# A feed-forward kernel with more groups by seven products and one sum made by an accumulating transfer

## The chip, the cores and the metric

The kernel runs on one core of a Trainium2 chip. The metric is the device time of one execution in microseconds (us). Times given as the median are over three executions without a profile; everything about engines comes from one further execution recorded by the hardware profiler. TensorE (PE) multiplies, VectorE (DVE) and ScalarE (ACT) work elementwise, GpSimd (POOL) and SyncE (SP) here issue transfers, and 16 DMA engines move the data.

## The reference, cut to what matters

Two layers on a 256 x 2048 activation in float32. The first has a gated delta-rule and a linear-recurrence mixer, the second two kinds of attention. Each layer ends in a feed-forward of inner width 5632:

```python
def rmsnorm(x, w):
    y = xf * lax.rsqrt(jnp.mean(xf * xf, axis=-1, keepdims=True) + NORM_EPS)
    return (y * w.astype(jnp.float32)).astype(x.dtype)

def swiglu(hn, w_gate, w_up, w_down):
    return (jax.nn.silu(hn @ w_gate) * (hn @ w_up)) @ w_down

def reference(x, ...):
    h = x
    for layer in range(DEPTH):
        h = h + (gdn_rglru_mixer if layer % 2 == 0 else fox_moba_mixer)(rmsnorm(h, ...), ...)
        h = h + swiglu(rmsnorm(h, ffn_norm[layer]), ffn_w_gate[layer], ffn_w_up[layer], ffn_w_down[layer])
    return rmsnorm(h, final_norm)
```

All weights are float32 in HBM and are read once.

## The kernel before, in words

**Precision.** A float32 operand is kept as two parts in the matmul's own format: `hi`, a cast on ScalarE, and `lo`, the rest, a subtraction on VectorE. A product takes three matmuls: hi by hi, hi by lo, lo by hi. `split` (L176) makes the two parts of a weight tile of 128 x 1024, which `load` (L166) brought by one 512 KB transfer on SP's queue. Raw tiles come from two pools, `wr` with three buffers and, in the feed-forward, `raw4` with four.

**Mixers.** `first` (L210) starts the program: it loads the first four weight columns with the input in ten pieces, and multiplies as they arrive. `wstat` and `xstat` run the later projections. Between them small tasks are advanced by `tick` (L156): a task started with `start(gen, pace)` gets its next step when `pace` ticks have passed. `lru_tile` (L640) is such a task, one for each of eight tiles of the recurrence.

**Feed-forward.** `ffn` (L482) runs eleven blocks of gate and up, 512 columns of each, in stages of four, four and three blocks. Behind each stage come two down blocks (`p` = 0 and 1) over the rows that the stage has produced. A `block` (L409) keeps four sums in PSUM, `F[t][i]`: two halves `t` of the 256 rows by two column groups `i` (gate and up, or two groups of h). Its inner dimension is cut into groups `m` of four 128-row tiles, and each group is computed in one of two ways:

- plainly: four weight tiles, each split, each used for both row halves; 48 matmuls of 128 x 512;
- by sevens (`seven`, L424), in the manner of Strassen and Winograd: seven products in place of eight, 42 matmuls. Three of its weight operands are loaded tiles b11, b22 and b21. Four are sums of loaded tiles: T1 = b11 + b12, T3 = b12 + b22, T2 = T1 + b22, T4 = T2 + b21. `total` (L372) makes a sum on VectorE, then its two parts. The activations' sums are made once by `combine` (L382) for a group and used by all blocks of a stage. Four further banks `M` take products that belong to more than one result, and `ends` (L449) joins them by four sums on VectorE when the last step of the sevens is done.

`groups` (L501) says how many groups of each gate and up block go by sevens: 0, 2, 2, 2 in the first stage, 2 in each later block. Every down block has one. Steps of `seven` are spread between plain units: `lead` and `trail` say how many plain units stand before the first and behind the last step. `hooks` are calls made before plain unit j: transposing the last block's result (`turn`), `combine`, the norm's `rstd`.

After a gate and up block, VectorE adds bank sums to F, ScalarE applies silu, VectorE multiplies, into tiles `fa`. After a down block VectorE adds to h.

**What sets the order.** A planning layer below the program text orders each engine's instructions by its own estimate of when operands are ready and buffers free; each queue then runs in that order. At the end of the last down block the order is written by hand (`second_half`, L1137): final norm, scaling, and output by column groups.

Of the kernel before, what the change touches and what calls it, by code (L numbers as in the profile page):

```python
# [10 lines left out]
D = 2048  # L11
# [36 lines left out]
def body(tc, A, out):  # L48
# [161 lines left out]
    def first(src, n, w):  # L210
# [8 lines left out]
        for a, b in [(k, k + 1) for k in range(4)] + [(k, k + 2) for k in range(4, NK, 2)]:  # L219
            nc.sync.dma_start(xw[a // 4][:, a % 4:a % 4 + b - a], src[:, a:b])  # L220
            if b == 12:
                nc.sync.dma_start(tab[:, 0:NTAB0], A["tab"][:, 0:NTAB0])
                nc.sync.dma_start(col[:, 16:], A["col"][:, 16:])
        for u in range(NK // 2):
            hi = wh.tile([128, 1024], F32R, name="whi")
            lo = wl.tile([128, 1024], F32R, name="wlo")
            for a, b in [(0, 1), (1, 2)] if u < 2 else [(0, 2)]:
                ks = range(2 * u + a, 2 * u + b)
                for k in ks:
                    x = xw[k // 4][:, k % 4, 0:T]  # L230
                    S.activation(X[:, k, 0], x, AF.Copy, scale=w[:, k:k + 1])
                    V.scalar_tensor_tensor(out=X[:, k, 1], in0=x, scalar=w[:, k:k + 1], in1=X[:, k, 0].bitcast(F32),
                                           op0=ALU.mult, op1=ALU.subtract)
                raw = xw[u // 2][:, u % 2 * 2 + a:u % 2 * 2 + b, T:]
                c = slice(512 * a, 512 * b)
                rows = lambda t: t[:, c].rearrange("p (k n) -> p k n", n=n * 128)
                if u == a == 0:
                    V.tensor_copy(rows(hi), raw)
                else:
                    S.copy(rows(hi), raw)  # L240
                V.tensor_sub(rows(lo), raw, rows(hi).bitcast(F32))
                for k in ks:
                    for i, P in enumerate(Ps):
                        ws = slice((k % 2 * n + i) * 128, (k % 2 * n + i + 1) * 128)
                        PE.matmul(P, hi[:, ws], X[:, k, 0], start=k == 0, stop=False)
                        PE.matmul(P, hi[:, ws], X[:, k, 1], start=False, stop=False)
                        PE.matmul(P, lo[:, ws], X[:, k, 0], start=False, stop=k == NK - 1)
# [65 lines left out]
    def sumsq(g, *ts):  # L313
        for t in ts or range(2):
            j = (mx.tile([128, 1024], F32, name="junk", tag="T", bufs=3)[:, 0:512] if more else
# [56 lines left out]
    def total(a, b, name):  # L372

        t = mx.tile([128, 1024], F32, name=name, tag="T", bufs=3)
        V.tensor_tensor(out=t, in0=a, in1=b, op=ALU.add)  # L375
# [4 lines left out]
        return t, (hi, lo)  # L380

    def combine(x4):  # L382

        f = mx.tile([128, 4, T], F32, name="cf", tag="T", bufs=3)
        c = mx.tile([128, 4, 2, 128], F32, name="cc4", tag="T", bufs=3)
        r = fp.tile([128, 2, 4, 2, 128], F32R, name="comb", tag="comb", bufs=3)
# [22 lines left out]
    def block(src, x, comb, nd, hooks, tail=0, lead=2, trail=None):  # L409
# [14 lines left out]
        def seven(m):  # L424
# [5 lines left out]
            yield  # L430
            b12 = load(src(1, 2 * m))
            t, w = total(b11, b12, "T1")
            M[1].add(cx(0), w)
# [12 lines left out]
            F[1][0].add(q(1, 1), total(t, b21, "T4")[1])  # L446
# [35 lines left out]
    def ffn(L, then, fin=None):  # L482
# [18 lines left out]
        for groups in ((0, 2, 2, 2), (2, 2, 2, 2), (2, 2, 2)):  # L501
# [3 lines left out]
            for j in range(piece):  # L505
# [5 lines left out]
                if j == 1 and piece == 3:  # L511
                    hooks.update(late)
                F, e = block(lambda i, u: gu[b, u, i], lambda k: X[:, k], {m: lambda m=m: cx[m] for m in range(groups[j])}, 4, hooks)
                a = [fp.tile([128, 512], F32, name=f"fa{t}", tag="fa", bufs=2) for t in range(2)]
                for t in range(2):
                    if e:
                        V.tensor_tensor(out=a[t], in0=F[t][0], in1=e[t][0], op=(ALU.add, ALU.subtract)[t])
                    S.activation(a[t], a[t] if e else F[t][0], AF.Silu, scale=nrm["rs"][:, t:t + 1])
                for t in range(2):
                    if e:  # L520
                        V.tensor_tensor(out=e[t][1], in0=F[t][1], in1=e[t][1], op=ALU.add)
                    V.scalar_tensor_tensor(out=a[t], in0=e[t][1] if e else F[t][1], scalar=nrm["rs"][:, t:t + 1], in1=a[t],
                                           op0=ALU.mult, op1=ALU.mult)
                    todo.append((hid, j, t, a[t]))
# [71 lines left out]
    def mixer0():  # L596
# [540 lines left out]
    def second_half(add):  # L1137
# [3 lines left out]

        def root(t):

            for i, o in ((2, z[t]), (3, x[t])):
                V.scalar_tensor_tensor(out=o, in0=ssp[:, t, i:i + 1], scalar=1.0 / D, in1=part[:, t:t + 1] if i == 2 else z[t],
                                       op0=ALU.mult, op1=ALU.add)
# [20 lines left out]
        add(1, 0)  # L1167
        root(0)
        sumsq(2, 1)
# [3 lines left out]
        sumsq(3, 1)  # L1173
        ready(0, 2)
        ready(0, 3)
        root(1)
        ready(0, 1)
# [99 lines left out]
```

## Time and profile before

| What | us |
|---|---|
| median of three executions | 2233.04 (2232.82 to 2233.43) |
| profiled execution, device time | 2232.51 |
| its span, first to last instruction | 2230.7 |
| TensorE busy | 2215.9 |
| VectorE busy | 1928.9 |
| ScalarE busy | 1278.9 |
| GpSimd busy | 2.1 |

The clock granted to TensorE was 0.999 of full speed. 420 MB came over SP's queue. The time outside the span is 1.8 us. In the profile's rows, L and a number is the line of the program that made the instruction, `x` and a number counts instructions, and `<-` separates what is written from what is read. For an idle time, `<-` names what ended it. "PEld" are TensorE's weight loads, which run beside its matmuls. Matmul rows overlap their neighbours, so the distance between two starts is the cost of one, not its duration.

### The profile page before, as it was taken

The numbers are of one execution on the slowest core, as the hardware profiler recorded it, in microseconds if no ns is written. First come the engines' busy times: TensorE is split into PE (matmuls) and PEld (weight loads), VectorE is DVE, ScalarE is ACT, GpSimd is POOL, SyncE is SP. The second block draws the span as 40 slices with busy tenths as digits, with TensorE's granted clock in tenths as the row PEclk, the third lists the DMA queues.
The fourth block names the chain that finished last, engine by engine and source line by source line (L and its number), as shares of the span: only waits on it lengthen the run. The fifth ranks groups of instructions, "written<-read, shape, count | busy, mean of one in ns | idle before, by whom it ended". The sixth has DMA issues, their size and how long they took to land.

```text
span 2230.7 us, 30096 instructions
## 1 busy us (share of the span) xinstructions
PE 2215.9 (99%) x11026; PEld 1852.0 (83%) x11026; DVE 1928.9 (86%) x2716; ACT 1278.9 (57%) x1670; POOL 2.1 (0%) x6
## 2 busy tenths in 40 slices
PE   9999999999999999999999999999999999999998
PEld 8888888888888888888878888888888888888886
DVE  8899676789989999899966658857999999999998
ACT  6776664565555665565654444445665466555565
POOL 0000000000000000000000000000000000000000
PEclk9999999999999999999999999999999999999999
DMA  7445445665565666656545455456665666666563
GB/s 280 161 144 168 140 150 187 214 208 195 192 215 196 201 195 203 207 187 200 180 158 175 158 172 172 162 186 217 208 198 191 208 205 203 194 210 202 181 219 131
DMA packets 117780, 422.29 MB, mean 189 GB/s; under 512 B 13152, under 2 KB 14688, under 8 KB 117504
## 3 DMA queue, kind: packets, MB, share of 16 engines
q1 hardware_dynamic: 117344, 420.10, 56.7%
q8 instruction: 86, 1.41, 0.2%
q14 instruction: 62, 0.51, 0.1%
q10 hardware_dynamic: 288, 0.27, 0.0%
HBM read 418.22 MB, written 2.10 MB: 188 GB/s over the span
## 4 chain that ended last, share of the span: by engine, by line
PE 97%; DVE 1%; DMA 1%; ACT 0%; issue 0%; SPq 0%; DVEq 0%; ACTq 0%
PE F L405 16%; PE F L406 16%; PE F L404 16%; PE Pw L199 11%; PE Pw L204 6%; PE Px L303 5%; PE Px L305 5%; PE Px L304 5%; PE M L404 4%; PE M L405 4%; PE M L406 4%; PE Ph L492 1%; PE Psc L1053 1%; PE Pt L326 0%; PE Ps L563 0%; DMA raw<-in_gu 0%
## 5 line engine op out<-in xcount | busy, mean ns | idle before, releaser
L179 ACT CAST whi<-raw 128x1024 fp32r<-128x1024 f32 x724 | 760.7, 1052 | 744.8 <-PE F L406 359.1
L180 DVE TENSOR_TENSOR wlo<-raw,whi 128x1024 fp32r<-128x1024 f32 x724 | 876.5, 1219 | 185.0 <-PE Px L304 74.0
L199 PE MATMUL Pw<-X,whi 128*128 128x512 f32 x1088 | 388.0, 400 | 0.0
L404 PE MATMUL F<-whi,X 128*128 128x512 f32 x848 | 330.5, 391 | 0.0
L405 PE MATMUL F<-wlo,X 128*128 128x512 f32 x848 | 330.4, 390 | 0.0
L406 PE MATMUL F<-whi,X 128*128 128x512 f32 x848 | 330.1, 389 | 0.0
L204 PE MATMUL Pw<-X,wlo 128*128 128x256 f32 x1088 | 304.7, 280 | 0.1
L378 ACT CAST thi<-T 128x1024 fp32r<-128x1024 f32 x208 | 219.1, 1054 | 98.6 <-DVE T L375 71.5
L379 DVE TENSOR_TENSOR tlo<-T,thi 128x1024 fp32r<-128x1024 f32 x208 | 252.5, 1219 | 24.7 <-ACT thi L378 24.2
L199 PEld LDWEIGHTS Pw<-X,whi 128*128 128x128 f32 x1088 | 204.1, 188 | 47.4 <-issue 0.5
L405 PE MATMUL F<-wlo,hid 128*128 128x512 f32 x536 | 208.9, 390 | 0.0
L406 PE MATMUL F<-whi,hid 128*128 128x512 f32 x536 | 208.7, 389 | 0.0
L404 PE MATMUL F<-whi,hid 128*128 128x512 f32 x536 | 208.6, 390 | 0.0
L204 PEld LDWEIGHTS Pw<-X,wlo 128*128 128x128 f32 x1088 | 205.4, 189 | 1.2 <-DVE wlo L180 0.7
L406 PEld LDWEIGHTS F<-whi,X 128*128 128x128 f32 x848 | 159.2, 188 | 33.1
L404 PEld LDWEIGHTS F<-whi,X 128*128 128x128 f32 x848 | 159.2, 188 | 32.7
L405 PEld LDWEIGHTS F<-wlo,X 128*128 128x128 f32 x848 | 159.3, 188 | 32.5
L375 DVE TENSOR_TENSOR T<-raw,raw 128x1024 f32<-128x1024 f32 x98 | 119.2, 1218 | 11.0 <-DMA raw<-in_gu 8.9
L375 DVE TENSOR_TENSOR T<-T,raw 128x1024 f32<-128x1024 f32 x104 | 126.6, 1218 | 1.9 <-DMA raw<-in_dn 1.7
L404 PE MATMUL M<-thi,comb 128*128 128x512 f32 x312 | 121.3, 391 | 0.6 <-ACT thi L378 0.6
L405 PE MATMUL M<-tlo,comb 128*128 128x512 f32 x312 | 121.6, 390 | 0.0
L406 PE MATMUL M<-thi,comb 128*128 128x512 f32 x312 | 121.5, 389 | 0.0
(385 smaller groups left out, 3217.1 us busy)
## 6 DMA issues: line engine op xcount, KB each, us to landing
raw<-in_gu SPq DMA_DIRECT2D x352, 512.0 KB, 4.1
raw<-in_dn SPq DMA_DIRECT2D x176, 512.0 KB, 4.3
raw<-in_w0w SPq DMA_DIRECT2D x72, 512.0 KB, 3.6
raw<-in_wo SPq DMA_DIRECT2D x64, 512.0 KB, 3.5
raw<-in_w1w SPq DMA_DIRECT2D x64, 512.0 KB, 3.6
raw<-in_w1x SPq DMA_DIRECT2D x32, 512.0 KB, 3.6
raw<-in_w0x SPq DMA_DIRECT2D x16, 512.0 KB, 3.6
xw<-in_xw SPq DMA_DIRECT2D x6, 768.0 KB, 10.9
```

The lines of the kernel that those rows point to most:

```text
L179: S.copy(hi, raw)
L180: V.tensor_sub(lo, raw, hi.bitcast(F32))
L199: PE.matmul(P.rearrange("p a b -> p (a b)"), hi[:, kk], X[:, k].rearrange("p a b -> p (a b)"), start=k == 0, stop=False)
L204: PE.matmul(P[:, 0], lo[:, kk], X[:, k, 0], start=False, stop=k == NK - 1)
L303: PE.matmul(Ps[t], x[:, 0, ts], hi[:, kk], start=k == 0, stop=False)
L304: PE.matmul(Ps[t], x[:, 0, ts], lo[:, kk], start=False, stop=False)
L375: V.tensor_tensor(out=t, in0=a, in1=b, op=ALU.add)
L378: S.copy(hi, t)
L379: V.tensor_sub(lo, t, hi.bitcast(F32))
L404: PE.matmul(self.t, xh, hi[:, kk], start=self.i == kk == 0, stop=False)
L405: PE.matmul(self.t, xh, lo[:, kk], start=False, stop=False)
L406: PE.matmul(self.t, xl, hi[:, kk], start=False, stop=kk == 1 and self.i == self.n - 1)
```

## The change

- One more group by sevens in the first gate and up block of each feed-forward (0 becomes 1), with `lead` 6 there; one more in the second down block behind each four-block stage, whose `combine` is called from the first down block's hook 9.
- T3 is no longer summed on VectorE. Once T1 has been formed, GpSimd's queue issues an accumulating transfer that adds b22 from HBM onto the tile of b12 in place; the tile is split later like the other sums. `total` becomes `halves`, which only splits. The other three sums run in one tile, `t`, and each is formed as soon as its operands allow: T1 ahead of the first yield, T2 and T4 right after the previous value has been split. b22 is still loaded and split as an operand.
- Two buffers in place of three for the tag `T`, four in place of three for `comb`. The tiles `fa` are gone: silu and product go into the bank sums' own tiles. First blocks, which had no bank sums, now have them.
- `first` brings the fifth and sixth weight tile as pieces of their own and splits them separately; the first `lru_tile` starts with a pace of 4; in the closing norm the two small sums are moved apart, so that the square root needs only the first.

```diff
-        for a, b in [(k, k + 1) for k in range(4)] + [(k, k + 2) for k in range(4, NK, 2)]:
+        for a, b in [(k, k + 1) for k in range(6)] + [(k, k + 2) for k in range(6, NK, 2)]:
...
-            for a, b in [(0, 1), (1, 2)] if u < 2 else [(0, 2)]:
+            for a, b in [(0, 1), (1, 2)] if u < 3 else [(0, 2)]:
...
-    def total(a, b, name):
-
-        t = mx.tile([128, 1024], F32, name=name, tag="T", bufs=3)
-        V.tensor_tensor(out=t, in0=a, in1=b, op=ALU.add)
+    def halves(t):
+
         hi = fp.tile([128, 1024], F32R, name="thi", tag="thi", bufs=2)
         lo = fp.tile([128, 1024], F32R, name="tlo", tag="tlo", bufs=2)
         S.copy(hi, t)
         V.tensor_sub(lo, t, hi.bitcast(F32))
-        return t, (hi, lo)
+        return hi, lo
...
             b11 = load(src(0, 2 * m))
             M[0].add(q(0, 0), split(b11))
-            yield
             b12 = load(src(1, 2 * m))
-            t, w = total(b11, b12, "T1")
-            M[1].add(cx(0), w)
+
+            t = mx.tile([128, 1024], F32, name="T", tag="T", bufs=2)
+            more_of = lambda a, b: V.tensor_tensor(out=t, in0=a, in1=b, op=ALU.add)
+            more_of(b11, b12)
+
+            G.dma_start(b12, src(1, 2 * m + 1), accum_op=ALU.add)
             yield
             b22 = load(src(1, 2 * m + 1))
             F[0][1].add(cx(3), split(b22))
             yield
-            M[3].add(cx(1), total(b12, b22, "T3")[1])
-            yield
-            t, w = total(t, b22, "T2")
-            M[2].add(cx(2), w)
+            M[1].add(cx(0), halves(t))
+            more_of(t, b22)
             yield
             b21 = load(src(0, 2 * m + 1))
             F[0][0].add(q(1, 0), split(b21))
             yield
-            F[1][0].add(q(1, 1), total(t, b21, "T4")[1])
+            M[2].add(cx(2), halves(t))
+            more_of(t, b21)
+            yield
+            M[3].add(cx(1), halves(b12))
+            yield
+            F[1][0].add(q(1, 1), halves(t))
             yield
...
-        for groups in ((0, 2, 2, 2), (2, 2, 2, 2), (2, 2, 2)):
+        for groups in ((1, 2, 2, 2), (2, 2, 2, 2), (2, 2, 2)):
...
-                    hooks.update(late)
-                F, e = block(..., 4, hooks)
-                a = [fp.tile([128, 512], F32, name=f"fa{t}", tag="fa", bufs=2) for t in range(2)]
+
+                    hooks[6] = late[4]
+                F, e = block(..., 4, hooks, lead=6 if b == 0 else 2, trail=2)
                 for t in range(2):
...
+                    V.tensor_tensor(out=e[t][0], in0=F[t][0], in1=e[t][0], op=(ALU.add, ALU.subtract)[t])
+                    S.activation(e[t][0], e[t][0], AF.Silu, scale=nrm["rs"][:, t:t + 1])
...
                 if p == 0 and piece == 4:
                     hooks.update(late)
+
+                    hooks[9] = lambda hid=hid: ch.update({1: combine(hid[:, 4:8])})
...
-                F, e = block(lambda i, u: dn[2 * p + i, u0 + u], lambda k: hid[:, k], {0: lambda: ch[0]}, piece, hooks, *last)
+                F, e = block(lambda i, u: dn[2 * p + i, u0 + u], lambda k: hid[:, k],
+                             {m: lambda m=m: ch[m] for m in range(1 + (p == 1 and piece == 4))}, piece, hooks, *last)
...
-            start(lru_tile(n, wstat(W[n], True), lw))
+            start(lru_tile(n, wstat(W[n], True), lw), 4 if n == 0 else 2)
...
+        def mean(t, i):
+
+            V.scalar_tensor_tensor(out=(z, x)[i][t], in0=ssp[:, t, 2 + i:3 + i], scalar=1.0 / D,
+                                   in1=z[t] if i else part[:, t:t + 1], op0=ALU.mult, op1=ALU.add)
+
         def root(t):
 
-            for i, o in ((2, z[t]), (3, x[t])):
-                V.scalar_tensor_tensor(out=o, in0=ssp[:, t, i:i + 1], scalar=1.0 / D, in1=part[:, t:t + 1] if i == 2 else z[t],
-                                       op0=ALU.mult, op1=ALU.add)
             S.activation(y[t], ssp[:, t, 3:4], AF.Sqrt, scale=1.0 / D, bias=z[t])
```

More of the change, by code (lines that the diff above doesn't have):

```diff
@@ L314, in sumsq @@
         for t in ts or range(2):
-            j = (mx.tile([128, 1024], F32, name="junk", tag="T", bufs=3)[:, 0:512] if more else
+            j = (mx.tile([128, 1024], F32, name="junk", tag="T", bufs=2)[:, 0:512] if more else
                  mx.tile([128, 512], F32, name="junk", tag="t2", bufs=4))
@@ L511, in ffn @@
                 if j == 1 and piece == 3:
[L512 to L514 removed]
+                    hooks[6] = late[4]
+                F, e = block(lambda i, u: gu[b, u, i], lambda k: X[:, k], {m: lambda m=m: cx[m] for m in range(groups[j])}, 4, hooks, lead=6 if b == 0 else 2, trail=2)
                 for t in range(2):
[L516 to L518 removed]
+                    V.tensor_tensor(out=e[t][0], in0=F[t][0], in1=e[t][0], op=(ALU.add, ALU.subtract)[t])
+                    S.activation(e[t][0], e[t][0], AF.Silu, scale=nrm["rs"][:, t:t + 1])
                 for t in range(2):
[L520 to L522 removed]
+                    V.tensor_tensor(out=e[t][1], in0=F[t][1], in1=e[t][1], op=ALU.add)
+                    V.scalar_tensor_tensor(out=e[t][0], in0=e[t][1], scalar=nrm["rs"][:, t:t + 1], in1=e[t][0],
                                            op0=ALU.mult, op1=ALU.mult)
[L524 removed]
+                    todo.append((hid, j, t, e[t][0]))
                 b += 1
@@ L1167, in second_half @@
         add(1, 0)
+        mean(0, 0)
         root(0)
+        mean(0, 1)
         sumsq(2, 1)
@@ L1173, in second_half @@
         sumsq(3, 1)
+        mean(1, 0)
         ready(0, 2)
@@ L1176, in second_half @@
         root(1)
+        mean(1, 1)
         ready(0, 1)
```

6 lines of the change are left out of this document (3 added, 3 removed).

## The prediction, made before the result was known

> **What bounds the kernel now.** The page's busy times and the chain that ended last come first: nearly the whole span is matmul work, one matmul behind the other.
>
> ```profile
> PE 2215.9 (99%) x11026; PEld 1852.0 (83%) x11026; DVE 1928.9 (86%) x2716; ACT 1278.9 (57%) x1670; POOL 2.1 (0%) x6
> ...
> PE 97%; DVE 1%; DMA 1%; ACT 0%; issue 0%; SPq 0%; DVEq 0%; ACTq 0%
> ```
>
> The shares are means over stages, so the feed-forward stage, where the change acts, is read by windows of 100 us. The columns are the window, then busy us and instructions of PE, PEld, DVE, ACT and POOL, then granted clock, DMA share and GB/s.
>
> ```profile
> 700.00:800.00 100.00, 99.60 (x448) 82.30 (x447) 96.42 (x96) 61.76 (x65) 0.00 (x0) 1.00 0.60 199
> 800.00:900.00 100.00, 100.00 (x451) 82.99 (x450) 96.82 (x104) 56.11 (x60) 0.00 (x0) 1.00 0.60 199
> 900.00:1000.00 100.00, 100.00 (x447) 82.89 (x446) 92.22 (x93) 54.60 (x55) 0.00 (x0) 1.00 0.60 201
> ```
>
> TensorE is never idle, but VectorE is 92 to 97% busy beside it: two engines at their limit. GpSimd does nothing, and the DMA engines are 60% busy. A busy matmul row says 0.39 us, but matmuls overlap, so the price of one is the distance between starts, in the timeline:
>
> ```profile
> 738.01 0.39 PE L404 MATMUL F<-whi,X 128*128 128x512 f32 x1
> ...
> 752.06 0.39 PE L406 MATMUL F<-whi,comb 128*128 128x512 f32 x1
> ```
>
> These are first and last of 63 matmuls, 62 steps in 14.05 us: 0.2266 us each. VectorE's work on a tile of 128x1024 is priced the same way:
>
> ```profile
> 744.10 1.23 DVE L180 TENSOR_TENSOR wlo<-raw,whi 128x1024 fp32r<-128x1024 f32 x1
> ...
> 753.19 1.22 DVE L379 TENSOR_TENSOR tlo<-T,thi 128x1024 fp32r<-128x1024 f32 x1
> ```
>
> That is first and last of nine in a row, eight steps in 9.09 us: 1.137 us each. How near VectorE is to holding TensorE up shows in a rare matmul that had to wait for it, and in the waits, where ScalarE by contrast mostly waits for TensorE to free a buffer (total us, times, longest):
>
> ```profile
> 759.87 0.50 PE L405 MATMUL F<-tlo,X 128*128 128x512 f32 x1 [0.40 <-DVE tlo L379]
> ```
>
> ```profile
> ACT whi L179 <- PE F L406: 359.1, 267, 3.3
> ...
> DVE T L375 <- DMA raw<-in_gu: 8.9, 13, 1.8
> ```
>
> **Six more groups by sevens.** A plain group is 4 tiles x 2 row halves x 6 = 48 matmuls, a group by sevens 7 x 6 = 42. The first block of each feed-forward gains one, and so does the second down block of each of its two four-block stages: 3 per feed-forward, 6 in all, 36 matmuls. TensorE loses 36 x 0.2266 = **8.16 us**. All of it is on the path, provided that the other engines keep up in these six blocks.
>
> **Does VectorE keep up?** These groups price its work (busy us, then mean ns of one):
>
> ```profile
> L378 ACT CAST thi<-T 128x1024 fp32r<-128x1024 f32 x208 | 219.1, 1054 | 98.6 <-DVE T L375 71.5 <-PE M L406 23.6 <-PE F L406 1.8
> L379 DVE TENSOR_TENSOR tlo<-T,thi 128x1024 fp32r<-128x1024 f32 x208 | 252.5, 1219 | 24.7 <-ACT thi L378 24.2
> ...
> L375 DVE TENSOR_TENSOR T<-T,raw 128x1024 f32<-128x1024 f32 x104 | 126.6, 1218 | 1.9 <-DMA raw<-in_dn 1.7
> L375 DVE TENSOR_TENSOR T<-raw,raw 128x1024 f32<-128x1024 f32 x98 | 119.2, 1218 | 11.0 <-DMA raw<-in_gu 8.9
> ...
> L453 DVE TENSOR_TENSOR e<-M,e 128x512 f32<-128x512 f32 x128 | 84.8, 683 | 1.7 <-PE M L406 1.4
> ...
> L539 DVE TENSOR_TENSOR e<-h,e 128x512 f32<-128x512 f32 x48 | 30.8, 682 | 0.0
> L546 DVE TENSOR_TENSOR h<-F,e 128x512 f32<-128x512 f32 x44 | 29.5, 683 | 1.3 <-PE F L406 1.3
> L522 DVE SCALAR_TENSOR_TENSOR fa<-e,rs,fa 128x512 f32<-128x512 f32 x40 | 29.0, 745 | 0.0
> ...
> L392 DVE TENSOR_TENSOR comb<-cc,comb 128x1024 fp32r<-128x1024 f32 x10 | 12.2, 1220 | 0.3
> ...
> L390 DVE TENSOR_TENSOR cc<-cf,cc 128x256 f32<-128x256 f32 x20 | 8.3, 417 | 0.0
> ```
>
> Before, a group by sevens has 3 splits, 4 sums and 4 splits of sums on VectorE: 11 x 1.137 = 12.5 us against 42 x 0.2266 = 9.5 us of matmuls. A plain group has 4 x 1.137 = 4.5 us against 10.9. So a group by sevens is VectorE's burden, paid for by plain groups beside it. The change takes one sum of the four to a transfer: 10 x 1.137 = 11.4 us.
>
> A block of two and two, by rows: before, (2 x 11 + 8) x 1.137 = 34.1 us, and 4 bank sums, 4 gate sums and 2 of the transposed result at some 0.60 (0.68 less the 0.08 by which 1.219 exceeds 1.137), and 2 gate products at 0.66: 7.3. Together 41.4 us, in a block that takes 42.4:
>
> ```profile
> 736.60 0.87 PE Ph L492 x8
> 778.99 0.87 PE Ph L492 x8
> ```
>
> That is 98%, as the windows say. After: 28 x 1.137 + 7.3 = 39.1 us, 92%. Second down block of a four-block stage, now two and two: 31.8 + 12 x 0.60 = 39.0 us against 180 x 0.2266 = 40.8. First down block, one and three, with both combines in it: 22 x 1.137 + 14 x 0.60 + 2 x (1.22 + 4 x 0.42 + 1.22) = 41.6 against 186 x 0.2266 + 1.7 of transposes = 43.9. First block, one and three: 25.0 + 7.3 - 1.2 + 2 x 4.1 + about 1 for the norm = 40.3 against 42.1. Each fits, by 4 to 5%, so I take no loss; what pays for it is the sums taken away. If these still went over VectorE, the down block would need 41.3 of 40.8.
>
> ScalarE gets three more casts per new group and four more of combine: 22 x 1.05 = 23 us. At 57% busy it has the room. The four combines' VectorE work is counted above.
>
> **The sum by a transfer.** 58 accumulating transfers of 512 KB are added on GpSimd's queue, which nothing else uses there. The transfer waits for the first sum (it overwrites an operand of it), and cast and subtraction of its result wait for it. Its price shows nowhere in the trace. The nearest rows:
>
> ```profile
> raw<-in_gu SPq DMA_DIRECT2D x352, 512.0 KB, 4.1
> raw<-in_dn SPq DMA_DIRECT2D x176, 512.0 KB, 4.3
> ```
>
> Lower end 4.1 us, a plain load of the size; upper end three of these, 12.3 us, for it reads HBM, reads SBUF and writes SBUF. I take 7 us, under two loads (8.2), because the engines are only 60% busy and the second stream is on chip.
>
> What hides it: the order of the changed program puts 8 to 27 VectorE instructions between the first sum and the subtraction that uses the transfer; at row prices 9.1 to 23.2 us, 16 of the 58 under 12. ScalarE's queue is stricter: behind the waiting cast stand casts of other tiles, which VectorE wants next. Counting the casts at 1.05 us each, the transfer must be in within 5.2 to 7.5 us in some 14 cases, within 10 in 18, and later in the other 40. At 7 us the overruns are at most 1.8 us each, in some nine blocks that each have 3.3 us to spare. So 0 on the path. If the cover goes, what is late next is ScalarE's cast, then every cast behind it, then TensorE.
>
> Traffic: 58 x 512 KB is 11% more in the two stages, 22% if each costs double: the DMA share goes from 0.60 to 0.73 at most. Plain loads share these engines and may land later. The changed order holds one raw buffer longer and another shorter; counting VectorE's work between a buffer's release and its next use, 18 of 528 loads have under 4 us, before 28. Taken at zero; above it stands the 8.9 us that VectorE already waited there, without TensorE stopping for more than the row quoted.
>
> [...]
>
> **Sums ahead of splits, one running sum, two T buffers, gate in place, hooks.** Same instructions in another order. A combine needs both T buffers, and every hook that calls one stands behind the last step of a group by sevens (position 9 or 10 after step 7 at 7 or 8; 6 after 4). Gate tiles are now the bank sums' own, read by the next block's transposes at unit 2, rewritten after unit 4. Cost 0, hidden by these distances.
>
> **Three small edits.**
>
> ```profile
> 12.12 0.38 PE L245 MATMUL Pw<-X,whi 128*128 128x256 f32 x1 [0.65 <-ACT whi L240]
> ...
> PE Pgate L645 <- ACT cx L582: 0.6, 1, 0.6
> ...
> 2221.77 1.41 DVE L1159 SCALAR_TENSOR_TENSOR fin<-h,fin,fin 128x512 f32<-128x512 f32 x2
> ...
> 2223.09 0.42 DVE L1145 SCALAR_TENSOR_TENSOR fin<-ssp,fin 128x1 f32<-128x1 f32 x2
> 2223.34 0.29 ACT L1147 ACTIVATE fin<-ssp,fin 128x1 f32<-128x1 f32 x1 [0.73 <-DVE fin L1145]
> ```
>
> Finer first pieces remove up to 0.65; two more casts and one more issue come back, so 0.4. The first recurrence tile's later step removes its 0.6. At the end the square root no longer waits 0.73 for two small sums that stand behind two products on VectorE; the products keep VectorE until 2223.1 anyway, so 0.3 of it. Together **1.3 us**.
>
> **The sum.** The profiled execution took 2232.5 us (span 2230.7 and 1.8 around it), 0.5 under the median of 2233.04. 2232.5 - 8.16 - 1.3 = 2223.0; set against the median 2223.6. I say **2223.6 us**.
>
> **Rivals.**
>
> *Late transfers: slower.* [...] At 12.3 us the 18 tight cases overrun by 5 us on average, 90 us; in some 14 blocks 3.3 each is absorbed, 46; 44 lost less the gain of 9.5: about 2268 us. [...] Against: GpSimd's queue is empty, and most uses stand 12 us and more away.
>
> *Late in part: a smaller gain.* At 8.5 us and loads at 5, some 4 us are lost: about 2227.5.
>
> *VectorE sets the pace: no change.* If the transfers cost VectorE some 0.05 us an instruction, its work in the down blocks passes TensorE's (40 x 0.05 makes 41.0 of its 39.0, against 40.8), and matmuls saved become waits: only the small edits stay, 2233.0 - 1.3, about 2231.7. For: four to five per cent of room. Against: 41.4 of 42.4 was fed without stops.
>
> **How the numbers follow.** A change of less than 0.2% (4.5 us) is about what a measurement of this kernel can't tell from none. My forecast, 2218 to 2227: 0.58. In part: 0.13. No change: 0.09. Slower: 0.20. So faster 0.71, same 0.09, slower 0.20. The likeliest case's own range is 2218 (a few more of the short waits gone) to 2227; the range reaches over the smaller gain, no change and the first of the slower, 2218 to 2240, and leaves the late transfers out.
>
> **What would show it.** Right: 36 matmuls fewer at the same 0.2266 us; PE idle no more than 15 us; VectorE nearer 92 than 97% in the gate blocks; accumulating transfers landing within 8 us; Pgate's wait gone. Wrong: waits of the cast of the transferred sum, PE waiting for such a cast, plain loads at 6 us or more, or VectorE rows above 1.22 us.

## The result and the profile after

The changed kernel takes **2246.61 us** (median of six, 2243.82 to 2247.91) where the kernel before takes 2233.19: a ratio of 1.0058, 95% interval 1.0045 to 1.0071. It is 13.4 us slower; 2223.6 was forecast, and 2240 was the end of the range. The profiled execution took 2246.88 us with a span of 2245.1.

The page after, busy times, then the chain that ended last, then GpSimd's data queue (packets, MB, share of 16 engines):

```profile
PE 2219.3 (99%) x10990; PEld 1842.4 (82%) x10990; DVE 1942.5 (87%) x2741; ACT 1294.9 (58%) x1695; POOL 52.3 (2%) x64
...
PE 91%; DVE 4%; DMA 3%; issue 1%; ACT 1%; DVEq 0%; ACTq 0%
...
q0 software_dynamic: 8352, 30.41, 8.2%
```

The 36 matmuls are gone (11026 to 10990), but the chain is no longer all TensorE: 97% has become 91%, and VectorE and loads stand in it. The windows shown of before, now:

```profile
700.00:800.00 100.00, 100.00 (x447) 81.62 (x446) 94.53 (x94) 60.92 (x65) 4.31 (x5) 1.00 0.76 229
800.00:900.00 100.00, 98.68 (x442) 80.93 (x441) 93.75 (x102) 55.11 (x58) 2.59 (x3) 1.00 0.69 214
900.00:1000.00 100.00, 99.40 (x438) 80.58 (x437) 95.30 (x97) 57.82 (x59) 5.17 (x6) 1.00 0.77 229
```

VectorE is a little less busy in two windows and more in the third, the DMA engines are at 0.69 to 0.77 in place of 0.60, and TensorE now loses up to 1.3 us of a window. Its waits for the subtraction of a sum (total us, times, longest), before and then after:

```profile
PE F L405 <- DVE tlo L379: 0.4, 1, 0.4
```

```profile
PE F L403 <- DVE tlo L377: 8.3, 10, 1.4
```

Beside these 8.3 us it waits 3.3 more in the feed-forward after the change, for the two parts of a plain tile. VectorE's sums wait for loads not much longer in all than the 8.9 us shown of before:

```profile
DVE T L431 <- DMA raw<-in_gu: 10.7, 10, 1.7
```

The landing times (KB, median us), where the loads of gate and up tiles had 4.1:

```profile
raw<-in_gu SPq DMA_DIRECT2D x352, 512.0 KB, 4.6
...
raw<-in_gu POOLq DMA_DIRECT2D x42, 512.0 KB, 6.7
```

By stage, from the first matmul of one to the first of the next, the span grew by 14.4 us. GU is a stage of gate and up blocks, DN the two down blocks behind it:

| After less before, us | GU 1 | DN 1 | GU 2 | DN 2 | GU 3 | DN 3 |
|---|---|---|---|---|---|---|
| matmuls saved, forecast | -1.36 | -1.36 | 0 | -1.36 | 0 | 0 |
| first feed-forward | +4.0 | +0.1 | +2.2 | -0.2 | +0.8 | 0.0 |
| second feed-forward | +2.9 | 0.0 | +2.4 | +0.5 | +1.9 | -1.1 |

Two places show how it is lost. The first is a block's end. Here is the timeline of SP, VectorE and TensorE there; the SPq row covers two load issues, the first at 678.92 and the last 10.3 us later. Then the chain that released VectorE's sum (start, us, what):

```profile
678.92 10.60 SPq L173 DMA_DIRECT2D raw<-in_gu  x2
...
680.11 1.23 DVE L431 TENSOR_TENSOR T<-raw,raw 128x1024 f32<-128x1024 f32 x1 [1.21 <-DMA raw<-in_gu]
...
681.85 1.22 DVE L377 TENSOR_TENSOR tlo<-T,thi 128x1024 fp32r<-128x1024 f32 x1
...
683.12 0.50 PE L403 MATMUL F<-tlo,hid 128*128 128x512 f32 x1 [0.92 <-DVE tlo L377]
```

```profile
674.09 1.15 DVE wlo L180
675.25 4.76 DMA raw<-in_gu
680.11 1.23 DVE T L431
```

The next block's first sum stands in VectorE's queue ahead of the last subtraction of this one; it waits 1.21 us for a load, and TensorE waits 0.92 for the subtraction. That load, of b12, was issued when the subtraction of an ordinary tile had freed its buffer, and took 4.76 us. Nine of the ten waits above, 8.0 of the 8.3 us, are this chain, each with such a load, of 4.1 to 5.2 us (median 4.8). In the kernel before the sum stands there at ten block ends, too, with loads of 3.5 to 4.5 (median 3.9); it waits at most 0.78, and TensorE stops once, for 0.40.

In the same stretch SP's queue issues nothing for 10.3 us, because its next buffer isn't free. SP's waits for a buffer, before and then after, show it in the longest of them:

```profile
SPq L173 <- DVE wlo L180: 1425.7, 571, 6.8
```

```profile
SPq L173 <- DVE wlo L180: 1375.0, 555, 10.1
```

Counted over the feed-forwards' load issues, none before was over 8 us behind the last; after there are eight. But each of the eight stands behind the buffer of an ordinary tile, when seven tiles of the next block are loaded already. They are no loss of lead.

The second place is the first block of a feed-forward, where only the three buffers of `wr` are in use for the first twelve loads:

```profile
447.65 11.60 SPq L173 DMA_DIRECT2D raw<-in_gu  x4
...
448.20 1.00 POOL L434 DMA_DIRECT2D raw<-in_gu  x1 [421.10 <-DMA raw<-in_gu]
...
456.59 1.04 ACT L179 CAST whi<-raw 128x1024 fp32r<-128x1024 f32 x1 [2.69 <-DMA raw<-in_gu]
```

```profile
450.45 6.06 DMA raw<-in_gu
```

```profile
457.68 0.50 PE L402 MATMUL F<-whi,X 128*128 128x512 f32 x1 [0.89 <-ACT whi L179]
458.94 0.50 PE L403 MATMUL F<-wlo,X 128*128 128x512 f32 x1 [0.76 <-DVE wlo L180]
...
459.91 0.63 PE L403 MATMUL F<-wlo,X 128*128 128x512 f32 x1
460.34 0.63 PE L404 MATMUL F<-whi,X 128*128 128x512 f32 x1
```

Four loads in 11.6 us. The one that the cast waits for was issued beside the transfer, as soon as an ordinary subtraction had freed one of the three buffers, and took 6.06 us; the load at this place in the second feed-forward took 6.7, and without transfers 3.5 and 3.7 (e1 below). The cast waits 2.69 for it, TensorE waits, and then runs 0.43 us a matmul for 3 us (the last section).

### The profile page after: what moved, and what is told of

It reads as the page before. It is cut to its first block, busy times and chain, and to the rows that moved or that the text cites. A ratio compares the mean times of both kernels' runs of the same rounds, so it can differ in the third digit from the quotient of the medians.

```text
span 2245.1 us, 30395 instructions
## 1 busy us (share of the span) xinstructions
PE 2219.3 (99%) x10990; PEld 1842.4 (82%) x10990; DVE 1942.5 (87%) x2741; ACT 1294.9 (58%) x1695; POOL 52.3 (2%) x64
## 4 chain that ended last, share of the span: by engine, by line
PE 91%; DVE 4%; DMA 3%; issue 1%; ACT 1%; DVEq 0%; ACTq 0%
PE F L403 14%; PE F L402 14%; PE F L404 14%; PE Pw L199 11%; PE Pw L204 5%; PE Px L303 5%; PE Px L305 5%; PE Px L304 5%; PE M L403 4%; PE M L402 4%; PE M L404 4%; DMA raw<-in_gu 3%; DVE wlo L180 1%; DVE T L431 1%; DVE tlo L377 1%; PE Ph L496 1%
## 5 line engine op out<-in xcount | busy, mean ns | idle before, releaser
L179 ACT CAST whi<-raw 128x1024 fp32r<-128x1024 f32 x718 | 750.5, 1052 | 687.6 <-PE F L404 329.7
L402 PE MATMUL F<-whi,X 128*128 128x512 f32 x820 | 321.6, 392 | 1.5 <-ACT whi L179 1.5
L404 PE MATMUL F<-whi,X 128*128 128x512 f32 x820 | 320.0, 390 | 0.0
L376 ACT CAST thi<-T 128x1024 fp32r<-128x1024 f32 x174 | 183.0, 1052 | 134.2 <-DVE T L431 97.0
L377 DVE TENSOR_TENSOR tlo<-T,thi 128x1024 fp32r<-128x1024 f32 x174 | 211.8, 1218 | 15.0 <-ACT thi L376 14.4
L402 PE MATMUL F<-whi,hid 128*128 128x512 f32 x480 | 187.6, 391 | 0.0
L404 PE MATMUL F<-whi,hid 128*128 128x512 f32 x480 | 187.0, 390 | 0.0
L403 PE MATMUL F<-wlo,hid 128*128 128x512 f32 x480 | 186.9, 389 | 0.0
L402 PEld LDWEIGHTS F<-whi,X 128*128 128x128 f32 x820 | 154.3, 188 | 32.6 <-ACT whi L179 2.3
L431 DVE TENSOR_TENSOR T<-T,raw 128x1024 f32<-128x1024 f32 x116 | 141.4, 1219 | 0.8
L404 PE MATMUL M<-thi,comb 128*128 128x512 f32 x348 | 135.4, 389 | 0.0
L402 PE MATMUL M<-thi,comb 128*128 128x512 f32 x348 | 135.4, 389 | 0.0
L403 PE MATMUL M<-tlo,comb 128*128 128x512 f32 x348 | 135.4, 389 | 0.0
L404 PEld LDWEIGHTS F<-whi,hid 128*128 128x128 f32 x480 | 90.1, 188 | 18.8
```

Source lines behind the costliest of these rows:

```text
L179: S.copy(hi, raw)
L376: S.copy(hi, t)
L377: V.tensor_sub(lo, t, hi.bitcast(F32))
L402: PE.matmul(self.t, xh, hi[:, kk], start=self.i == kk == 0, stop=False)
L403: PE.matmul(self.t, xh, lo[:, kk], start=False, stop=False)
L404: PE.matmul(self.t, xl, hi[:, kk], start=False, stop=kk == 1 and self.i == self.n - 1)
```

## The experiments

All times are medians; the ratio is to runs of the kernel before made beside them.

| Run | us | ratio, 95% interval |
|---|---|---|
| changed kernel | 2246.61 | 1.0058, 1.0045 to 1.0071 |
| e1 sum on VectorE | 2237.51 | 1.0019, 1.0009 to 1.0028 |
| e2 counts as before | 2255.88 | 1.0097, 1.0082 to 1.0112 |
| e3 first block plain | 2243.31 | 1.0044, 1.0029 to 1.0058 |
| e4 seven buffers earlier | 2241.12 | 1.0035, 1.0020 to 1.0049 |
| e5 = e1 and e4 | 2232.06 | 0.9994, 0.9985 to 1.0004 |
| e6 = e5, steps in the old order | 2235.55 | 1.0009, 1.0000 to 1.0018 |
| e7 transfers without sum | 2241.59 | 1.0040, 1.0025 to 1.0054 |
| e8 = e5, first block plain | 2237.04 | 1.0016, 1.0007 to 1.0025 |
| e10 = e5, transfers in the third stage | 2234.06 | 1.0001, 0.9991 to 1.0010 |
| e12 before, small edits alone | 2233.62 | 1.0000, 0.9991 to 1.0009 |
| e13 = e4, transferred sum used earlier | 2282.23 | 1.0215, 1.0202 to 1.0229 |
| e14 = e5, combine early in third block | 2239.30 | 1.0024, 1.0014 to 1.0033 |
| e15 = e5, combine late in third block | 2231.47 | 0.9991, 0.9982 to 1.0000 |
| e16 = e5, groups as before | 2241.91 | 1.0036, 1.0023 to 1.0050 |
| e17 = e16, idle transfers | 2242.70 | 1.0041, 1.0026 to 1.0056 |
| e18 = e5, buffer held longer | 2239.06 | 1.0033, 1.0020 to 1.0046 |
| e21 transfers, groups as before | 2251.39 | 1.0088, 1.0073 to 1.0103 |
| e20 = e21, target off the rings | 2236.92 | 1.0021, 1.0011 to 1.0031 |

**One part undone at a time.** The first theory (A in the expectations) was that the transfers and their late loads lose the time; its rival, that the added groups overload VectorE and ScalarE.

```diff
 e1
-            G.dma_start(b12, src(1, 2 * m + 1), accum_op=ALU.add)
 ...
             F[0][1].add(cx(3), split(b22))
+            V.tensor_tensor(out=b12, in0=b12, in1=b22, op=ALU.add)
 e3 (and e2, which also takes the second group from the down blocks)
-        for groups in ((1, 2, 2, 2), (2, 2, 2, 2), (2, 2, 2)):
+        for groups in ((0, 2, 2, 2), (2, 2, 2, 2), (2, 2, 2)):
 e4
-        loads[0] = -12
+        loads[0] = -4
```

> The changed kernel with T3 summed on VectorE again, in place on the tile of b12, and no accumulating transfers; all else stays. Theory A (late loads: the transfers' traffic and the long hold on b12's buffer make weight tiles land late, and a sum or cast that waits for one holds up its whole queue): the stalls go with the transfers, 2224 to 2236 us, though VectorE works 58 x 1.14 = 66 us more. Theory B (VectorE is short of time in the blocks that gained a group): more work on VectorE makes it worse, 2250 us or more.

> The changed kernel with the number of groups by sevens as before: none in the first blocks, one in every down block. The transfers (52 of them), the order of the sums and the small edits stay. Theory A: the first blocks' loss of about 9.7 us is gone, the down blocks' 6 us of gain and 6 of loss cancel, about 2240 us, so still above the kernel before. Theory B: 2233 us or less, for VectorE then has less to do than in the kernel before.

> The changed kernel with plain first blocks; the second down blocks keep their two groups by sevens. Theory A: the first blocks' stages took 4.0 and 2.9 us longer than before though each has 6 matmuls less; without them 2239 to 2241 us. Theory B: the down blocks are the burden, at most 2 us less than the changed kernel, 2244 us or more.

> The changed kernel with the four buffers of raw4 in use from the fifth load of each feed-forward and not from the thirteenth, so that the first block's group by sevens has seven raw buffers and not three. Theory A: the first blocks' stalls of 3 to 5 us each go, and with them the half clock behind them, 2237 to 2240 us. Theory B: no effect, within 1 us of 2246.6.

Putting the sum back on VectorE gains 9.1 us, although VectorE gets 58 instructions more, and the four down stages with two groups in their second block now take 0.75 to 1.4 us less than before: these groups pay. Using the four buffers of `raw4` from the fifth load on gains 5.5. Both times lie just above theory A's ranges (by 1.5 and 1.1 us) and far from its rival's (e1), or between the two (e4). The first blocks' groups cost 3.3 us with the transfers (e3, between the two expectations). e2 missed on both: taking the down blocks' second group away, too, made 12.6 us *more*, lost in single waits of up to 5.2 us in the first block of the second stages. So fewer groups by sevens are no repair, and that wait is taken up below.

**Both repairs, the order, and half the traffic.** e5 joins e1 and e4; e6 has the old order of steps with sums in place; e7 leaves the accumulation out of the transfer; e8 is e5 with a plain first block.

```diff
 e7
-            G.dma_start(b12, src(1, 2 * m + 1), accum_op=ALU.add)
+            G.dma_start(b12, src(1, 2 * m + 1))
 e6
             M[0].add(q(0, 0), split(b11))
+            yield
             b12 = load(src(1, 2 * m))
             ...
+            M[1].add(cx(0), halves(t))
             yield
             b22 = load(src(1, 2 * m + 1))
             F[0][1].add(cx(3), split(b22))
             yield
+            V.tensor_tensor(out=b12, in0=b12, in1=b22, op=ALU.add)
+            M[3].add(cx(1), halves(b12))
+            yield
             more_of(t, b22)
+            M[2].add(cx(2), halves(t))
             ...
```

> VectorE forms b12+b22 and the fourth raw buffer ring is in use from the fifth load on. If the two repairs mend different places, their gains add: 2246.6 - 9.1 (sum on VectorE) - 5.5 (ring earlier) = about 2232 (2230 to 2234). If they mend the same place (casts of the first block waiting for a load), little is added to the first of them: 2234 to 2237.

> As the run with both repairs, but each group's steps in the order of before (every sum formed just ahead of its own split, sums in place, no transfers). If the order of the steps (a next block's first sum ahead of the last step's subtraction in VectorE's queue) is what the third stage loses, the stages of gate and up come back from +1.8 and +3.4 us against before to about 0 and the whole comes to 2222 to 2228. If the order is harmless and VectorE simply has too much to do with one more group per stage, it stays within 1.5 us of the run with both repairs.

> The changed kernel with transfers that copy and do not accumulate (b12 then holds b22 alone, so the third middle sum is left out of the result): the same 58 issues, waits, buffers and landings' order, but half the traffic if accumulating reads the target too. If the loss by the transfers is DMA engine time (3.2 us of 16 engines each, against 1.6), their share of the engines halves and the time lies half way to the run with the sum on VectorE: 2239 to 2243. If it is the buffer that they hold and the wait for their landing, it stays at 2245 to 2248.

> As the run with both repairs, but the first block of each feed-forward layer without a group by sevens (two groups fewer, 12 matmuls or 2.7 us more). If the groups in the first blocks pay as matmuls saved, 2.7 us above the run with both repairs. If they cost what they save there (casts and sums at a block whose loads have only begun), within 1 us of it or below.

The two gains add (14.6 us), but by stages they overlap: the first stages, at +4.0 and +2.9 in the changed kernel, are at +0.7 and +1.0 in e1, +1.3 and +0.2 in e4, +0.6 and -0.2 in e5. That they mend different places isn't shown. The old order is 3.5 us slower, outside both expectations: without transfers, sums ahead of splits are no fault of the change; beside transfers this doesn't show it. The first blocks' groups, a loss of 3.3 us in the changed kernel, are worth 5.0 here, more than the 2.7 of their matmuls; the rest isn't explained. Without the accumulation the transfer takes 4.1% of the engines in place of 8.2%, lands in 4.7 us in place of 6.7, and 5.0 us come back, as expected of traffic.

**Traffic or the held buffer?** From the start of the sum b11 + b12 to the end of the subtraction of the transferred sum, b12's raw buffer is held 19.1 us in the changed kernel (median of the 56 groups whose sum is in the trace), as long in e7, and 11.5 in e1. So e7's gain came without a shorter hold. The transfer itself lands a median of 8.5 us before its cast starts. How long SP's queue stands behind that buffer can be read: a load into it waits for the transferred tile's subtraction (L377). The changed kernel, then e5, which has no transfers:

```profile
SPq L173 <- DVE tlo L377: 72.3, 56, 3.4
```

```profile
SPq L173 <- DVE tlo L377: 133.8, 56, 4.3
```

The queue stands behind it for less time in all than without transfers, at most 3.4 us at once. e13 tests the hold all the same and moves the use of the sum forward, on the base of e4. e12 and e10 settle two smaller terms.

```diff
 e13
             M[1].add(cx(0), halves(t))
             more_of(t, b22)
             yield
+            M[3].add(cx(1), halves(b12))
+            yield
             b21 = load(src(0, 2 * m + 1))
             ...
-            M[3].add(cx(1), halves(b12))
-            yield
 e10 (block gets dma = piece == 3)
+            if dma:
+                G.dma_start(b12, src(1, 2 * m + 1), accum_op=ALU.add)
 ...
+            if not dma:
+                V.tensor_tensor(out=b12, in0=b12, in1=b22, op=ALU.add)
```

> The changed kernel with the early ring, and the step that splits the transferred sum moved ahead of the load of b21, so that its raw buffer is free some two steps sooner. The traffic is the same. If SP's queue standing behind that held buffer is what makes the loads late, the issue gaps over 8 us go and the time falls from 2241.1 to 2234 to 2238. If the traffic alone does it, 2240 to 2242.

> VectorE forms b12+b22 and the ring of raw buffers starts early as before in these runs, but the six groups of each third stage (12 of 58) use the accumulating transfer. In the third stage VectorE lost 2.8 and 2.0 us against before, and the kernel with transfers and the early ring only 0.2 and 0.3. If a transfer helps where VectorE is the limit and costs elsewhere, 2232.1 - 2.6 - 1.7 = 2227.8 (2226 to 2229.5). If transfers cost wherever they stand, 2232 or more.

> The kernel before with the small edits alone (finer first pieces, first recurrence tile at pace 4, the closing norm's small sums moved apart). By the prediction 1.3 us: 2231.8. By the trace of the changed kernel (start 0.8 later, the gate's wait moved to another producer, 0.2 at the end) nothing: 2233.1 to 2233.9.

e13 missed both expectations, by 40 us. The hold fell to 13.9 us and the long issue gaps from nine (e4) to two, but now the casts stand for the landing. ScalarE's waits of e13; the changed kernel has no row of this kind:

```profile
ACT thi L376 <- DMA raw<-in_gu: 134.8, 31, 6.4
```

So the hold can't be shortened this way: it is the cover of the landing, and the run can't part the two theories. e10 lies in the second range expected of it, 2232 or more: in the third stages it lost 4.4 and 2.0 us against before, no less than e5, mostly in `PE F L402 <- ACT thi L376` (3.2 us in all); why the transfers help there in e4 and not here was not found. The small edits alone are worth nothing.

**Traffic alone, and the hold taken away.** e16 is e5 with the groups as before and three `comb` tiles, which leaves room for a tile that nothing reads; e17 adds accumulating transfers into it, each behind the same first sum. e21 is e16 without the marker and with the real transfers; e20 gives b12 two tiles of its own, so that SP's queue never meets a raw buffer that a transfer holds; it also adds two buffers to the seven, and no run adds buffers without taking b12 off the rings.

```diff
 e16 and e17
             more_of(b11, b12)
+            V.tensor_copy(scr[0][:, 0:1], t[:, 0:1])
 e17 only
+            G.dma_start(scr[0], src(1, 2 * m + 1), accum_op=ALU.add)
 e20 against e21
-            b12 = load(src(1, 2 * m))
+            b12 = mx.tile([128, 1024], F32, name="b12", tag="b12", bufs=2)
+            nc.sync.dma_start(b12, src(1, 2 * m))
```

> Groups as before (no group in the first blocks, one in every down block), VectorE forms b12+b22 in place, early ring, the steps in the new order, and one VectorE copy of a 128x1 column per group as a marker. Baseline for the run beside it. The two runs with both repairs put the down groups at -1.1 to -1.4 us in each of four stages: 2237.0 + 5 = about 2242 if nothing else moves; 2233 to 2236 if the order of steps costs nothing against before.

> The run beside it with an accumulating transfer of 512 KB per group (52) into a tile that nothing reads, issued behind the marker, at the place where the changed kernel issues its own. Buffers and steps are the same; only traffic and GpSimd's issues are added. If traffic makes plain loads late and TensorE wait, 4 to 10 us above the run beside it, with plain loads at 4.9 us or more beside a transfer. If only the raw buffer held longer costs, within 1 us of it.

> Groups as before, accumulating transfers into the loaded tile of b12, early ring. The baseline for the next run. Between the run with counts as before (2255.9) and that less the early ring's gain of up to 5.5: 2248 to 2256.

> The same, with b12 in two tiles of its own, outside the seven raw buffers that SP's queue fills in turn. Transfers, traffic and waits for their landing stay; what goes is that a load in SP's queue waits for the buffer that a transfer holds. If that held buffer is the cost, the time falls to that of the idle transfers, 2240 to 2244, with no issue gaps over 8 us. If the use of the transferred sum is the cost, it stays within 2 us of the run beside it.

Windows of e16, then of e17:

```profile
700.00:800.00 100.00, 100.00 (x448) 81.89 (x447) 96.35 (x101) 60.22 (x64) 0.00 (x0) 1.00 0.62 197
```

```profile
700.00:800.00 100.00, 100.00 (x448) 81.92 (x448) 96.46 (x101) 60.63 (x65) 4.33 (x5) 1.00 0.76 223
```

The same 0.76 of the DMA engines as in the changed kernel, plain loads later in the mean of the feed-forwards (4.3 to 4.6 us), and TensorE not idle. The two medians differ by 0.8 us, within their intervals. Traffic alone is not the cause; but here the first sum stands ahead of the last subtraction at two block ends only, in the changed kernel at ten. With b12 off the rings, 14.5 us come back, to 2236.92: below the 2240 to 2244 expected, and 5.0 below e16, which has no transfers at all. So this edit takes away more than the transfers cost, and its gain is no measure of a held buffer. TensorE's waits in the feed-forward, all of them, of e21:

```profile
PE F L402 <- ACT thi L376: 8.3, 3, 4.0
...
PE F L403 <- DVE tlo L377: 2.7, 4, 1.3
```

and of e20:

```profile
PE M L403 <- DVE tlo L377: 0.6, 1, 0.6
```

Where the longest of these arises, in windows of 5 us, e21 first, then e20 at the same work, from one window earlier:

```profile
700.00:705.00 5.00, 5.00 (x24) 4.08 (x22) 3.33 (x3) 1.06 (x1) 0.00 (x0) 1.00 0.95 248
705.00:710.00 5.00, 1.04 (x4) 0.62 (x3) 0.74 (x1) 2.76 (x3) 0.00 (x0) 0.84 0.65 261
```

```profile
695.00:700.00 5.00, 5.00 (x24) 4.14 (x23) 3.30 (x4) 2.88 (x3) 0.00 (x0) 1.00 1.00 261
700.00:705.00 5.00, 5.00 (x23) 4.01 (x22) 3.42 (x3) 3.93 (x4) 0.00 (x0) 1.00 0.91 361
705.00:710.00 5.00, 5.00 (x23) 3.94 (x22) 4.34 (x5) 2.37 (x4) 0.00 (x0) 1.00 0.23 54
```

The DMA engines saturate in both (0.95 and 1.00), when loads follow close behind an accumulating transfer; those loads then take 6.2 to 8.6 us in both. In e20 TensorE still has tiles ahead of it: the load of b21 was issued at 691.83 and took 4.3. In e21 it was issued at 698.52, when an ordinary tile's subtraction had freed its buffer, took 8.6, and TensorE stops for 4 us. e2's waits of up to 5.2 us stand at the same work. The changed kernel has no stop of this length.

Late landings that cost nothing elsewhere reach TensorE where the loads have no lead. In the changed kernel that is at two places. In the first blocks, the early ring (e4) cuts the first stages' losses of 4.0 and 2.9 us to 1.3 and 0.2 (its second stages lose 3.6 and 5.8 in place of 2.2 and 2.4), and half the transfers' engine time under the same hold (e7) cuts them to 1.1 and 0.3. At the block ends, 8.0 us of waits are the chain shown above. TensorE's waits for a sum's subtraction fall from 8.3 to 5.9 us in e7; e1, where no first sum stands ahead of a last subtraction, has none of the chain. (e1's 9.1 us come from both places, less 4.6 that its third stages lose more.) There the sum's place alone costs little (0.4 us in the kernel before; 0.6 in e20, where it stands so at 23 block ends), and later loads alone cost nothing that can be told (e17: 0.8 us, within the intervals). Why the planner puts the sum there, and how much of each stop is the later landing, was not measured.

**Holding longer without a transfer, and the third stage.** e18 puts the split of b12 + b22 last. e14 and e15 move the third stage's `combine`, which the change had moved to unit 6 of the second block.

```diff
 e18
-            M[3].add(cx(1), halves(b12))
-            yield
             F[1][0].add(q(1, 1), halves(t))
             yield
+            M[3].add(cx(1), halves(b12))
+            yield
 e15 (e14: hooks[1])
-                if j == 1 and piece == 3:
+                if j == 2 and piece == 3:
                     hooks[6] = late[4]
```

> The run with both repairs, without transfers, and the split of b12+b22 moved behind the last sum's, so that b12's raw buffer is held one step longer. If a held buffer alone makes loads late and TensorE wait, 2235 to 2242 with issue gaps over 8 us. If it takes the transfer as well, 2231 to 2233.

> The run with both repairs (sum on VectorE, early ring), and in the third stage the combine for the down blocks called before unit 1 of the third block instead of unit 6 of the second. If that combine, standing among the bank sums at the end of the second block, is what the third stage loses (2.8 and 2.0 us against before), the time falls by about 4 to 2228 (2227 to 2229.5). If the order of the steps loses it, 2231 to 2233.

> The same with the combine before unit 6 of the third block, again at the end of a block. If a place at the end of a block is what costs, no gain: 2231 to 2233. If only the second block was the wrong one, 2228.

e18 came out at the time that a held buffer would give, with seven long issue gaps, but its trace doesn't support the reading. VectorE's rows there:

```profile
1019.63 1.51 DVE L523 TENSOR_TENSOR e<-F,e 128x512 f32<-128x512 f32 x2
1021.05 1.22 DVE L390 TENSOR_TENSOR comb<-cc,comb 128x1024 fp32r<-128x1024 f32 x1
```

A weight's subtraction stands behind bank sums and the combine, and TensorE waits 3.1 us for it, once in each third stage: 6.2 of its 7.1 us of waits in the feed-forward. The planner had ordered VectorE otherwise, and none of TensorE's waits goes back to a load, though b12's buffer is held 19.4 us, as long as in the changed kernel. A hold without a transfer didn't make loads late for TensorE here.

e5 loses 2.8 and 2.0 us in the third stages. With the combine at the end of the third block it is 1.9 and 0.9; the median gains 0.6 us, as much as can be told from none. At that block's start it costs 7.2 us, which neither expectation had: the end of a block as such is not the bad place, though e15's time lies in the range named for that. What the third stages still lose was not settled. e15, the fastest run here, is 0.9991 of before, 0.9982 to 1.0000: a kernel with all the added groups and no transfer comes out even.

## Why the prediction was wrong

**The step that failed** is in *The sum by a transfer*: "Plain loads share these engines and may land later", taken at zero, because "above it stands the 8.9 us that VectorE already waited there, without TensorE stopping for more than the row quoted". The loads do land later, a median of 4.6 us in place of 4.1, and VectorE's waits for them grow only to 10.7 us. But the step took such waits as harmless wherever they fall. At nine block ends they now fall on a sum directly ahead of the subtraction that TensorE is due, and it stops for 8.0 us in all; the row quoted was the one such stop of before, 0.40. Taking the transfers out brought 9.1 us, first blocks included (e1). The same paragraph's count of a raw buffer held longer was no fault: it is held 19.1 us in place of 11.5 (e1), and SP's queue stands behind it 72 us in place of 134 (e5). *Sums ahead of splits* took the order at "Cost 0, hidden by these distances" and looked at the combines and gate tiles, not at this sum. The split of the 8.0 us between the landing and the order stays open.

**"Each fits, by 4 to 5%, so I take no loss"** failed for the first block: it priced VectorE and ScalarE and not the three buffers there, which give a load of 6.1 to 6.7 us no lead. With the early ring the two first stages get 5.5 us back (e4).

**"If these sums still went over VectorE, the down block would need 41.3 of 40.8"** was too dark: in e5, with these sums on VectorE, the four stages still gain 1.05 to 1.36 of the 1.36 us forecast. The transfers were not needed there.

**Matmuls**: right, 36 fewer at 0.2266 us. In the first stages e5 takes +0.6 and -0.2 us against before, e15 -0.3 and -1.0.

**The transfer's price**: right. 7 us were taken, 6.7 measured, and no cast waited for one. **Traffic at zero**: right by itself (e17: 0.8 us, within the intervals), wrong where the later loads have no lead.

**Small edits, 1.3 us**: zero (e12). In the changed kernel's one profiled execution the first matmul came at 5.52 us, before at 4.74, in e12 at 4.81; the finer pieces brought nothing. The gate's wait only moved to another producer:

```profile
PE Pgate L650 <- ACT V L837: 0.8, 1, 0.8
```

**Hooks at cost 0**: the combine at unit 6 of the second block costs some 2 us by stages (e5 to e15), though the median moves by 0.6 only, which can't be told from none.

**Rivals.** Late transfers was not the case: none of the changed kernel's casts waited for one. In e13 they did, and it took 41 us more than e4. That 44 were forecast is chance, for that was for a landing of 12.3 us, and the transfers of e13 landed in 6.8. VectorE's rows stayed at 1.22 us, so no cost of the transfers to VectorE shows. Nor does a delay of GpSimd's transfers beside a busy VectorE: in e4 all 58 issue 1.5 to 1.8 us after the first sum begins, which itself takes 1.22, and in the changed kernel, whose VectorE is 94 to 95% busy in the windows shown, 56 do so within 2.1 (median 1.75).

**The sum again.** From 2246.6 the sum on VectorE and the early ring together take 14.6 (e5), the combine 0.6 (e15): 2231.5. To 2223.6 remain 7.9: 1.3 of small edits, some 2.8 still lost in e15's third stages, 1.5 in its first stages and 0.9 in its down stages against the matmuls saved there, and 1.1 in its first mixer (all by its one profiled execution). The rest is no more than the runs of before vary.

## What to carry to other kernels

The transfers' price here was their landing (6.7 us) and their traffic (8.2% of the DMA engines), but also what the traffic did to loads that had no lead: 9.1 us came back without the transfers (e1). A sum of waits says little: beside 8.9 us of VectorE's waits for loads TensorE stopped for 0.40 (before), beside 10.7 for 8.0 (after). Ask what stands behind each of them in its engine's queue, and how soon TensorE needs that. Later loads cost nothing that could be told where the lead was there (e17: 0.8 us, within the intervals), so look first where it is short: at the start of a ring with few buffers (5.5 us back in e4), and where a load is issued just ahead of its use. A long gap between issues in the loading queue is no sign of loss by itself: the changed kernel's eight gaps over 8 us each had seven tiles loaded already. Read which buffer it waits for. The time that covered a transfer also held its buffer: at 13.9 us in e13, in place of 19.1 in the changed kernel, casts waited for the landing.

## What the runs showed of the hardware

After some stops TensorE ran slower for a while. In e21 it waited 3.96 us and then ran at 0.427 us a matmul, in place of 0.2266:

```profile
709.28 0.80 PE L402 MATMUL F<-thi,X 128*128 128x512 f32 x1 [3.96 <-ACT thi L376]
709.88 0.63 PE L402 MATMUL F<-whi,X 128*128 128x512 f32 x1
710.30 0.63 PE L403 MATMUL F<-wlo,X 128*128 128x512 f32 x1
710.73 0.63 PE L404 MATMUL F<-whi,X 128*128 128x512 f32 x1
```

It stayed so for 12 matmuls (5 us, 2.4 lost); after stops of 3.4 to 5.3 us in e2 and e18 it was 7 or 8. The changed kernel ran so from 459.91, for 3 us, with no single stop over 1.1 us, after three that add to 2.6 us within 5.6; the clock granted to TensorE was 0.50 of full speed from 460 to 462, 1.00 before 459 and after 463. Which stops bring this and which don't, the runs don't show.

An accumulating transfer of 512 KB took 3.2 us of the 16 engines (8.2% of the span for 58), the same without accumulating 1.6 (4.1%, e7), and VectorE's instructions kept their 1.22 us beside 58 of them.
